# A hybrid encoder layer on one core: a planner that charges engines for a change of start partition, with loops by halves and a new table

## The chip, the cores and the metric

The kernel runs on 1 core of a Trainium2 chip, as one program in one launch. The metric is the device time of that program in microseconds, as the median over several executions. Times of single instructions come from one profiled execution.

## The reference

One layer of a streaming encoder is computed for two request groups that share the weights: a prompt of 512 new frames and 32 further frames of a running stream with 1,024 cached keys. Both are stacked to 544 token columns, D_MODEL is 1024, everything is float32.

```python
xn = _rms_norm(x, p['norm1'])
q, k, v, iq, ik, iw, u, g_a, g_b = _split(xn @ p['w_in'], IN_SPLITS)
ik = _layer_norm(ik, p['idx_k_g'], p['idx_k_b'])
o_a = attend(q, iq, iw, k, v, ik)                       # top-256 (prompt: 128) keys by index score, softmax attention
y_b, shift_new, wkv_new = _rwkv_time_mix(u, shift_prev, wkv0, p)   # 8 heads, matrix state, one delta-rule step per token
merged = sigmoid(g_a) * (o_a @ p['w_oa']) + sigmoid(g_b) * (y_b @ p['w_ob'])
h = x + merged @ p['w_out']
hn = _rms_norm(h, p['norm2'])
h = h + (silu(hn @ p['w_gate']) * (hn @ p['w_up'])) @ p['w_down']
y = _rms_norm(h, norm_f)
```

The keys, values, index keys, the final matrix states and the last projected row are outputs too.

## The kernel before

All products with weights run as three matmuls each: weights and activations are split into a rounded high part and a low rest (`hi`, `lo`), and `hi*hi`, `hi*lo`, `lo*hi` are summed in PSUM (`gemm`, L279; the feed-forward's last product, L1332). `wblock` (L255 to L260) loads a block of weights of 512 KB by DMA from SP's queue, makes `hi` on ACT (L256) and `lo` on DVE (L260). Two raw buffers and three split buffers turn round. Token columns are handled in two halves of 272.

Before the feed-forward, small work with long chains of dependences lies between these products:

- The prologue (L296 to L341) loads the eight tiles of x, splits each (ACT L300, DVE L301), squares it (ACT L309), sums the squares (DVE L311, PE L316 and L317) and makes the normalised, split x. The first weight blocks, 24 and 25, are multiplied by x before it is normalised.
- `kv` projects keys and values, normalises the index keys (DVE, to L406) and transposes them (PE L432).
- `rwkv_prep` (P0 to P3, one for each pair of heads) makes from projected rows the operands of the delta rule. Two heads share the 128 partitions: head 0 (`e` = 0) lies in partitions 0 to 63, head 1 in 64 to 127, and many instructions of 64 or 32 partitions work on one half.
- `chain_step` (C0 to C3, nine steps for each pair) goes PE L1060, copies of its result by DVE (L1061, partitions from 0) and ACT (L1062, from 64), PE L1063, copies by DVE (L1064) and ACT (L1065), PE L1066, DVE L1069 or L1073, then the next step. All of a chain uses one PSUM bank, bank 7. At its end L1096 and L1099 make the outputs in the same bank, which ACT empties (L1100, L1102).
- `prompt_index` and `sample_index` (X, SI) find the top keys, `attend_prompt` and `attend_sample` (A, AS) attend to them.

No engine's order is that of the source. `build` writes the program once in the order of `ORDER`, `plan` takes from it the instructions, their dependences and a priority for each, to which the table `SHIFT` adds an offset by group (a group is a step of `ORDER`, its weight blocks have a "w" ahead of the name), and `schedule` runs a list planner: it keeps a time for each engine, a duration for each instruction (`cost`), a delay from engine to engine (`HOP`), a rule for the array of PE (`Array`), and always takes the ready instruction of the lowest priority number. The order that comes out is what `program` builds the second time, with every wait as the dependences require. `SHIFT` also has "hold" and "keep", which are added to the priority of matmuls that use the array in another shape than the last one.

```python
best = min(((h[0][0] + (extra if x != array.shape else 0), x) for x, h in tiles.items() if h), default=None)
...
k = heapq.heappop(here[e])[1]
...
end = free[e] = began + work[k]
...
r = began if e == engine[s] == "PE" else end + HOP[e, engine[s]]
```

Of the kernel before, what the change touches and what calls it, by code (L numbers as in the profile page):

```python
# [35 lines left out]
def _consts():  # L36
# [34 lines left out]
SHIFT = {  # L71
# [7 lines left out]
    "wstart": -38300,  # L79
# [77 lines left out]
class Kernel:  # L157
# [646 lines left out]
    def rwkv_prep(self, P):  # L804
# [46 lines left out]
        for src, pc, ts in pieces(kn):  # L851
            pv = PB[:, pc, ts]
            for e in range(2):
                ps = heads[e][1]
                nc.vector.scalar_tensor_tensor(at_slot(AR, pc, ts, e)[ps], src[ps], -1.0, pv[ps], op0=OP.mult, op1=OP.mult)
        for src, pc, ts in pieces(r):
            nc.vector.tensor_tensor(at_slot(AR, pc, ts, 2), src, PB[:, pc, ts.start + 1:ts.stop + 1], op=OP.mult)
        for (src, pc, ts), (iv, _, _) in zip(pieces(tm), pieces(pi)):
            for e, ps, _ in heads:
                nc.vector.scalar_tensor_tensor(at_slot(BK, pc, ts, e)[ps], src[ps], 0.5, iv[ps], op0=OP.mult, op1=OP.mult)  # L860
# [34 lines left out]
        for cs in ([0], [1, 2, 3, 4], [5, 6, 7, 8]):  # L895
# [8 lines left out]
            for e, ps, po in heads:  # L904
# [10 lines left out]
                if cs[0]:  # L915
                    pq = slice(64 * e, 64 * e + 32)
                    nc.scalar.activation(M21[pq, u0:u0 + n], bv[pq, :, ac + 32:ac + 64], AF.Copy)
# [552 lines left out]
def unlayout(r):  # L1470
# [8 lines left out]
HOP = {("PE", "Activation"): 200, ("PE", "DVE"): 200, ("PE", "Pool"): 225, ("DVE", "PE"): 149, ("Activation", "PE"): 123, ("Pool", "PE"): 174,  # L1479
       ("Activation", "DVE"): 142, ("DVE", "Activation"): 128, ("DVE", "Pool"): 155, ("Activation", "Pool"): 170, ("Pool", "Activation"): 75,  # L1480
       ("Pool", "DVE"): 70, ("DVE", "DVE"): 127, ("Pool", "Pool"): 104, ("Activation", "Activation"): 60, ("PE", "PE"): 0}
SECOND = {"PE": 54, "Activation": 70, "DVE": 70, "Pool": 48, "SP": 0}
ENGINES = ("PE", "Activation", "DVE", "Pool", "SP")
# [11 lines left out]
def cost(i):  # L1495
# [19 lines left out]
    if engine == "Pool":  # L1515
        if i.opcode == "TensorTensor":
            spread = any(st == 0 and c > 1 for st, c in list(a[1].ap)[1:]) or (a[0].ap == a[1].ap and str(a[0])[:30] == str(a[1])[:30])
# [3 lines left out]
    if i.opcode == "StreamTranspose":  # L1521
        return 1.95 * n
# [5 lines left out]
    return (0.521 if half else 1.042) * n + 68 + (61 if len(aps) > 3 or (len(aps) == 3 and wide == 2 and n > 1) else 0)  # L1528

# [66 lines left out]
def plan(K, instructions):  # L1596
# [25 lines left out]
    return L, group, prio, succ, need, engine, dma, work, bundles(succ, group, engine, work, reach)  # L1622
# [24 lines left out]
def schedule(L, group, prio, succ, need, engine, dma, work, runs):  # L1647
# [6 lines left out]
    hold, keep = SHIFT.get("hold", 0), SHIFT.get("keep", 0)  # L1654
    names = [e for e in ENGINES if e in engine]
    free, order, here = dict.fromkeys(names, 0.0), {e: [] for e in names}, {e: [] for e in names}
# [6 lines left out]
    array, queue, bus, left = Array(), 0.0, 0.0, len(L)  # L1663
# [22 lines left out]
    while left:  # L1686
# [3 lines left out]
        while coming and coming[0][0] <= t + 1e-6:  # L1690
# [3 lines left out]
            else:  # L1694
                heapq.heappush(here[engine[k]], (prio[k], k))
        for e in names:
            while (here[e] or e == "PE") and free[e] <= t + 1e-6:
# [83 lines left out]
```

## Time and profile before

| what | value |
|---|---|
| median of 3 runs | 1024.93 us (1021.34 to 1025.96) |
| profiled execution, its own time | 1024.11 us |
| its span, first to last instruction | 1022.3 us |
| PE busy | 976.9 us, 96% of the span |
| DVE busy | 632.0 us, 62% |
| ACT busy | 461.4 us, 45% |
| POOL busy | 185.9 us, 18% |
| mean DMA rate | 110 GB/s over the span |

PE is the matmul engine, PEld its weight loads, DVE the vector engine, ACT the scalar engine, POOL GpSimd; SP issues nearly all DMAs. Busy time is the union of an engine's instructions. An instruction's record reaches from its start to the acknowledged write of its result, so the records of neighbours on one engine can overlap. "Idle before" is the time since the engine's last record ended, and the name behind an arrow is the instruction whose end let it go on.

### The profile page before, as it was taken

The page shows a single profiled execution, that of the slowest core. Times are in us where ns is not written, and L with a number is a line of the kernel's source. Part 1 is how long each engine was busy: PE and PEld are TensorE (multiplying, and loading weights), DVE is VectorE, ACT ScalarE, POOL GpSimd, SP SyncE. Part 2 cuts the span into 40 slices and gives each one's busy share as a digit, 9 for nine tenths or more (in the row PEclk, how much of TensorE's full clock was granted, in tenths as well). Part 3 has the DMA queues.
Part 4 walks back from the last instruction along what each step waited for, and adds up shares of the span by engine and source line. Part 5 has one row for each costly group of instructions (what it writes and reads, how often), then busy time and mean ns, then how long its engine had stood idle before and what let it go on. Part 6 is the DMA issues. An engine that isn't in the chain of part 4 may idle for free.

```text
span 1022.3 us, 20851 instructions
## 1 busy us (share of the span) xinstructions
PE 976.9 (96%) x8268; PEld 926.3 (91%) x8268; DVE 632.0 (62%) x1452; ACT 461.4 (45%) x965; POOL 185.9 (18%) x307
## 2 busy tenths in 40 slices
PE   6999999999989899999999999999999999999996
PEld 6989987888788788898889999999999999999995
DVE  6857536889989889799868564444444444323232
ACT  6643554665554686466644443223322233223231
POOL 2213113323232331031000131111111111001112
PEclk9999999999999999999999999999999999999998
DMA  6335332324143437442446422222233222232322
GB/s 231 91 116 185 105 99 72 115 99 142 42 137 113 133 98 209 129 118 75 145 142 179 170 83 83 83 94 93 83 85 100 85 83 83 73 98 77 95 73 88
DMA packets 63283, 112.58 MB, mean 110 GB/s; under 512 B 13617, under 2 KB 33873, under 8 KB 63057
## 3 DMA queue, kind: packets, MB, share of 16 engines
q1 hardware_dynamic: 62144, 110.72, 35.4%
q8 instruction: 65, 1.06, 0.4%
q10 hardware_dynamic: 1040, 0.52, 0.2%
q14 instruction: 34, 0.27, 0.1%
HBM read 93.67 MB, written 17.14 MB: 108 GB/s over the span
## 4 chain that ended last, share of the span: by engine, by line
PE 55%; DVE 7%; ACT 3%; issue 1%; DMA 0%; POOL 0%; SPq 0%; DVEq 0%; ACTq 0%
PE bank L279 38%; PE bank L1332 13%; DVE f L616 1%; DVE f L611 1%; DVE f L615 1%; PE bank L661 1%; DVE w L260 1%; PE bank L670 1%; PE bank L458 1%; DVE f L645 0%; DMA f<-gate_dram 0%; ACT f L649 0%; ACT f L604 0%; PE bank L459 0%; ACT k L452 0%
## 5 line engine op out<-in xcount | busy, mean ns | idle before, releaser
L279 PE MATMUL bank<-r,w 128*128 128x272 f32 x4752 | 653.9, 292 | 2.5 <-DVE f L1196 1.4
L279 PEld LDWEIGHTS bank<-r,w 128*128 128x128 f32 x4752 | 614.3, 189 | 9.4 <-issue 1.8
L256 ACT ACTIVATE w<-raw 128x1024 fp32r<-128x1024 f32 (+2 forms) x135 | 137.5, 1021 | 230.6 <-PE bank L279 173.8
L260 DVE TENSOR_TENSOR w<-raw,w 128x1024 fp32r<-128x1024 f32 (+2 forms) x135 | 176.4, 1308 | 95.9 <-ACT w L256 95.5
L1332 PE MATMUL bank<-r,w 128*128 128x272 f32 x1056 | 133.0, 288 | 0.0
L1332 PEld LDWEIGHTS bank<-r,w 128*128 128x128 f32 x1056 | 132.4, 188 | 0.0
L1310 POOL TENSOR_TENSOR f<-f 128x544 f32<-128x544 f32 x22 | 30.4, 1382 | 233.9 <-DVE f L1307 224.9
L1307 DVE TENSOR_TENSOR f<-bank,f 128x272 f32<-128x272 f32 x44 | 19.4, 441 | 74.8 <-PE bank L279 74.8
L1300 DVE TENSOR_TENSOR f<-bank,f 128x272 f32<-128x272 f32 x44 | 19.1, 435 | 45.0 <-PE bank L279 45.0
L458 PE MATMUL bank<-k 128*128 128x512 f32 (+5 forms) x102 | 37.8, 378 | 4.0 <-ACT f L604 2.9
L453 POOL TENSOR_TENSOR k<-f,k 64x512 fp32r<-64x512 f32 (+1 forms) x22 | 29.6, 1345 | 61.1 <-ACT k L452 55.2
L1334 DVE TENSOR_TENSOR f<-bank,f 128x272 f32<-128x272 f32 x16 | 7.1, 441 | 48.1 <-PE bank L1332 48.1
L611 DVE SCALAR_TENSOR_TENSOR f<-f,f 128x256 f32<-128x256 f32 (+2 forms) x45 | 31.8, 707 | 3.4 <-ACT f L604 2.4
L459 PE MATMUL bank<-k 128*128 128x512 f32 (+5 forms) x102 | 33.0, 332 | 0.0
L1336 ACT ACTIVATE f<-f 128x272 f32<-128x272 f32 x16 | 6.8, 423 | 57.5 <-DVE f L1334 57.5
L279 PE MATMUL bank<-k,w 128*128 128x272 f32 x144 | 25.3, 341 | 7.4 <-ACT k L300 6.2
L1338 POOL TENSOR_TENSOR f<-f 128x272 f32<-128x272 f32 x13 | 12.1, 934 | 111.1 <-ACT f L1336 103.0
L1301 ACT ACTIVATE f<-f 128x272 f32<-128x272 f32 x44 | 18.6, 424 | 30.0 <-DVE f L1300 30.0
L1252 POOL TENSOR_TENSOR f<-f 128x272 f32<-128x272 f32 x14 | 12.5, 894 | 108.0 <-ACT f L1250 108.0
L458 PEld LDWEIGHTS bank<-k 128*128 128x128 f32 x102 | 19.0, 188 | 13.8 <-ACT f L604 5.2
L279 PEld LDWEIGHTS bank<-k,w 128*128 128x128 f32 x144 | 23.2, 232 | 8.9 <-ACT k L300 6.2
L1076 POOL COPY f<-f 64x64 f32<-64x64 f32 x56 | 16.4, 294 | 66.8 <-DVE f L1073 64.9
(352 smaller groups left out, 1247.7 us busy)
## 6 DMA issues: line engine op xcount, KB each, us to landing
raw<-in_w_x_dram SPq DMA_DIRECT2D x41, 512.0 KB, 3.5
raw<-in_w_gate_dram SPq DMA_DIRECT2D x22, 512.0 KB, 3.6
raw<-in_w_up_dram SPq DMA_DIRECT2D x22, 512.0 KB, 3.6
raw<-in_w_down_dram SPq DMA_DIRECT2D x16, 512.0 KB, 3.6
gate_dram<-f SPq DMA_DIRECT2D x16, 272.0 KB, 2.5
raw<-in_w_oa_dram SPq DMA_DIRECT2D x8, 512.0 KB, 4.0
raw<-in_w_out_dram SPq DMA_DIRECT2D x8, 512.0 KB, 4.2
f<-iq_dram SPq DMA_DIRECT2D x26, 128.0 KB, 3.0
```

The source lines that it names most:

```text
L256: nc.scalar.activation(hi[:, a], raw[:, a], AF.Copy)
L260: self.lo_eng.tensor_tensor(lo[:, b], raw[:, b], hif[:, b], op=OP.subtract)
L279: nc.tensor.matmul(o, a[:, k], c[k][:, s], start=n == 0, stop=n == 3 * nk - 1)
L453: nc.gpsimd.tensor_tensor(ql[0:64], raw[0:64], qh_r.v(512)[0:64, :n], op=OP.subtract)
L458: nc.tensor.matmul(out, q[0][:, i:i + m], self.KS[:, j, keys], start=True, stop=False)
L459: nc.tensor.matmul(out, q[1][:, i:i + m], self.KS[:, j, keys], start=False, stop=stop)
L611: nc.vector.scalar_tensor_tensor(acc, r[:, i * S:(i + 1) * S], w, acc, op0=OP.mult, op1=OP.add)
L1300: nc.vector.tensor_tensor(t1[:, s], o, self.rs[:, s], op=OP.mult)
L1301: nc.scalar.activation(t1[:, s], t1[:, s], AF.Silu)
L1307: nc.vector.tensor_tensor(t2[:, s], o, self.rs[:, s], op=OP.mult)
L1310: nc.gpsimd.tensor_tensor(t1, t1, t2, op=OP.mult)
L1332: nc.tensor.matmul(o, a[:, k], c[k0 + k][:, s], start=m == 0, stop=m == 65)
```

## The change

- `side` gives the partition at which an instruction's output starts. `schedule` keeps the last such partition for ACT, DVE and POOL (`at`), and adds `TURN` (128, 110 and 112 ns) to an instruction's time where it differs. Ready instructions are kept in one heap for each side; an extra offset "turn" for another side exists in the code, but the table has no such entry, so it is 0.
- Delays from ACT to PE, ACT to POOL and POOL to ACT are raised. The planner's duration of a DVE transpose falls from 1.95 ns to 1.05 ns a column plus 84, and one form of POOL's multiplication is no longer taken as cheap.
- Three loops of `rwkv_prep` run over the partition halves first: the outputs to `AR` by half 0, then half 1, those to `BK` by half 1, then half 0, and the copy to `M21` behind the first copy of its half.
- All offsets of `SHIFT` are new (two lines of it stand for the table).

```diff
 SHIFT = {
-    "A0": 302900, "A1": -69100, "A2": 1141800, "A3": -1027600, "AS": -334800, "C0": 205900, "C1": -554900, "C2": -13000,
+    "A0": 230600, "A1": -4400, "A2": -703900, "A3": -225600, "AS": -582700, "C0": 247900, "C1": -1362900, "C2": -248200,
...
-    375100, "R1": -279800, "R2": -224600, "R3": 7200, "S": -56600, "SI": 103300, "U0": 10100, "U1": 1219400, "U2": 195800,
+    "R0": 299400, "R1": -1861400, "R2": -142400, "R3": 126400, "S": -59800, "SI": 126900, "U0": -21700, "U1": 1680300, "U2":
...
-        for src, pc, ts in pieces(kn):
-            pv = PB[:, pc, ts]
-            for e in range(2):
-                ps = heads[e][1]
+        for e, ps, _ in heads:
+            for src, pc, ts in pieces(kn):
+                pv = PB[:, pc, ts]
                 nc.vector.scalar_tensor_tensor(at_slot(AR, pc, ts, e)[ps], src[ps], -1.0, pv[ps], op0=OP.mult, op1=OP.mult)
...
-        for (src, pc, ts), (iv, _, _) in zip(pieces(tm), pieces(pi)):
-            for e, ps, _ in heads:
+        for e, ps, _ in heads[::-1]:
+            for (src, pc, ts), (iv, _, _) in zip(pieces(tm), pieces(pi)):
...
-                if cs[0]:
-                    pq = slice(64 * e, 64 * e + 32)
-                    nc.scalar.activation(M21[pq, u0:u0 + n], bv[pq, :, ac + 32:ac + 64], AF.Copy)
+                    if cs[0] and sh == 0:
+                        nc.scalar.activation(M21[pq, u0:u0 + n], bv[pq, :, ac + 32:ac + 64], AF.Copy)
...
-HOP = {("PE", "Activation"): 200, ("PE", "DVE"): 200, ("PE", "Pool"): 225, ("DVE", "PE"): 149, ("Activation", "PE"): 123, ("Pool", "PE"): 174,
-       ("Activation", "DVE"): 142, ("DVE", "Activation"): 128, ("DVE", "Pool"): 155, ("Activation", "Pool"): 170, ("Pool", "Activation"): 75,
+HOP = {("PE", "Activation"): 200, ("PE", "DVE"): 200, ("PE", "Pool"): 225, ("DVE", "PE"): 149, ("Activation", "PE"): 160, ("Pool", "PE"): 174,
+       ("Activation", "DVE"): 142, ("DVE", "Activation"): 128, ("DVE", "Pool"): 155, ("Activation", "Pool"): 210, ("Pool", "Activation"): 250,
+TURN = {"Activation": 128, "DVE": 110, "Pool": 112}
...
-        return 1.95 * n
+        return 1.05 * n + 84
...
+def side(i):
+
+    a = next((x for x in i.outs if hasattr(x, "ap")), None)
+    step = list(a.ap)[0][0] if a is not None else 0
+    return a.offset // step if step else 0
...
-                    k = heapq.heappop(here[e])[1]
+                    best = min(((h[0][0] + (turn if x != at[e] else 0), x) for x, h in here[e].items() if h), default=None)
+                    if best is None:
+                        break
+                    k = heapq.heappop(here[e][best[1]])[1]
...
+                    if sides[k] != at[e]:
+                        began += TURN[e]
+                        at[e] = sides[k]
                     end = free[e] = began + work[k]
```

The same instructions remain on every engine, the number of changes of PE's array shape is 150 before and 149 now, and the changes of an output's start partition go from 142 to 126 on DVE, from 235 to 231 on ACT and from 92 to 94 on POOL. From the product with `w_ob` on (`merge`, the second half of the span) the engines' orders are the same but for a few neighbours. Three places where the order moved (code from L1060 on has numbers lower by 2 in the changed file):

**SP's queue at the start of the program.** `raw` is a weight block, half of one where it says 128x512, x_t the eight tiles of x, cache_keys keys that a later step needs. Before:

```order
L225 DMA f_58<-in_vec_dram 128x80
L255 DMA raw<-in_w_x_dram 128x512
L296 DMA f_58<-in_x_t_dram 128x544 x4
L298 DMA f_58<-in_consts_dram 128x494
L255 DMA raw<-in_w_x_dram 128x512
L296 DMA f_58<-in_x_t_dram 128x544 x4
L439 DMA f_74<-in_cache_keys_dram 128x512 x2
L255 DMA raw<-in_w_x_dram 128x1024
```

Now:

```order
L255 DMA raw<-in_w_x_dram 128x1024
L439 DMA f_74<-in_cache_keys_dram 128x512 x2
L225 DMA f_58<-in_vec_dram 128x80
L255 DMA raw<-in_w_x_dram 128x512
L296 DMA f_58<-in_x_t_dram 128x544 x4
L298 DMA f_58<-in_consts_dram 128x494
L255 DMA raw<-in_w_x_dram 128x512
L296 DMA f_58<-in_x_t_dram 128x544 x4
```

The second weight block (512 KB) and two pieces of the key cache (256 KB each) moved ahead of everything that the first products need. On ACT, the square of a tile (L309) now often stands ahead of its split (L300), and on PE the first sum of squares (L316) stands behind 43 products of the first two blocks instead of 58.

**PE in a step of chain C1** (bank_89 is bank 7, the chain's; L279 are the products that stand between). Before:

```order
L279 MATMUL bank_83<-r_70,w 128x272 x2
L1063 MATMUL bank_89<-f_58,f_74 128x64
L279 MATMUL bank_83<-r_70,w 128x272
L1066 MATMUL bank_89<-f_74 128x128
L279 MATMUL bank_83<-r_70,w 128x272 x3
```

Now:

```order
L1061 MATMUL bank_89<-f_58,f_74 128x64
L530 LDWEIGHTS f_74
L530 MATMUL bank_86<-f_74 128x2
L279 MATMUL bank_82<-r_70,w 128x272 x8
L1064 MATMUL bank_89<-f_74 128x128
L279 MATMUL bank_82<-r_70,w 128x272 x4
```

Between the chain's second and third matmul of this step stand 8 products where 1 stood.

**PE at the end of chain C2**, where the outputs' second group of blocks begins (L1096, now L1094) and needs the bank that ACT is emptying. Before:

```order
L1099 MATMUL bank_89<-f_58,f_74 64x64 x2
L458 MATMUL bank_84<-k 128x256
L459 MATMUL bank_84<-k 128x256
L279 MATMUL bank_83<-r_70,w 128x272
L279 MATMUL bank_82<-r_70,w 128x272 x3
L1096 MATMUL bank_89<-f_74,f_58 64x128 x2
```

Now:

```order
L1097 MATMUL bank_89<-f_58,f_74 64x64 x4
L1094 MATMUL bank_89<-f_74,f_58 64x128
L1097 MATMUL bank_89<-f_58,f_74 64x64 x2
L279 MATMUL bank_82<-r_70,w 128x272 x13
L1094 MATMUL bank_89<-f_74,f_58 64x128 x2
```

Between the two groups stand 13 products where 4 and two score matmuls stood.

## Rows read from the trace of the kernel before

**Rows 1.** Stretches: length; busy (instructions) of PE, PEld, DVE, ACT, POOL; clock; DMA share; GB/s.

```profile
0.00:25.00 25.00, 17.04 (x97) 15.24 (x98) 15.93 (x28) 17.03 (x26) 6.70 (x26) 0.95 0.68 234
...
233.00:306.00 73.00, 67.61 (x706) 60.15 (x704) 66.31 (x233) 39.48 (x100) 22.41 (x54) 0.98 0.34 104
306.00:414.00 108.00, 100.89 (x951) 89.80 (x949) 97.44 (x265) 71.19 (x188) 27.25 (x51) 1.00 0.46 142
...
538.00:1000.00 462.00, 462.00 (x3686) 461.86 (x3685) 204.87 (x286) 144.69 (x226) 55.99 (x50) 1.00 0.31 95
1000.00:1022.30 22.30, 12.56 (x105) 12.08 (x103) 5.54 (x16) 3.53 (x8) 5.45 (x7) 0.86 0.30 101
sum 1022.30, PE 976.93 PEld 926.30 DVE 631.96 ACT 461.37 POOL 185.94; mean PE 122.12 PEld 115.79 DVE 78.99 ACT 57.67 POOL 23.24
```

**Rows 2.** Waits of PE: who waited for whom, us in total, times, longest.

```profile
PE bank L1066 <- ACT f L1065: 4.5, 9, 0.9
PE bank L1063 <- ACT f L1062: 3.0, 4, 1.3
...
PE bank L432 <- DVE f L406: 2.4, 2, 1.9
PE bank L1096 <- ACT f L1102: 1.8, 3, 1.1
...
PE bank L1060 <- DVE f L1073: 1.4, 1, 1.4
```

**Rows 3.** Timeline, all engines, 280.5 to 283 us: start, duration, instruction.

```profile
280.23 0.43 PE L1063 MATMUL bank<-f,f 128*128 128x64 f32 x2
...
281.31 0.22 ACT L1065 ACTIVATE f<-bank 64x64 f32<-64x64 f32 x1
...
281.55 0.49 ACT L762 ACTIVATE f<-bank,f 128x272 f32<-128x272 f32 x1
...
281.58 0.49 PE L1066 MATMUL bank<-f 128*128 128x128 f32 x2 [0.73 <-ACT f L1065]
```

**Rows 4.** Timeline, all engines, 393.3 to 396 us.

```profile
394.83 0.25 ACT L1102 ACTIVATE f<-bank 32x128 f32<-32x128 f32 x1
...
395.13 0.44 PE L1096 MATMUL bank<-f,f 128*64 128x128 f32 x4 [1.12 <-ACT f L1102]
```

**Rows 5.** Timeline of DVE alone, 476.5 to 479 us.

```profile
476.73 0.29 DVE L1069 SCALAR_TENSOR_TENSOR f<-f,f,bank 64x64 f32<-64x64 f32 x1
477.05 0.09 DVE L616 MATCH_VALUE_LOAD f<-f 128x8 f32 x1
477.15 0.69 DVE L616 MATCH_REPLACE8 f<-f 128x512 f32<-128x512 f32 x1
477.76 0.16 DVE L650 RECIPROCAL f<-f 128x2 f32<-128x2 f32 x1
477.94 0.56 DVE L645 CUSTOM_DVE_ANT_0 f<-bank,f 128x384 f32<-128x384 f32 x1
```

**Rows 6.** Stretches of the start (columns as in the first group).

```profile
0.00:3.00 3.00, 0.00 (x0) 0.00 (x0) 0.67 (x8) 1.49 (x2) 2.26 (x19) 1.00 0.26 73
3.00:6.00 3.00, 0.00 (x0) 0.00 (x0) 1.12 (x3) 1.25 (x2) 1.59 (x3) 1.00 0.94 307
6.00:9.00 3.00, 2.82 (x9) 2.30 (x10) 1.96 (x3) 2.51 (x5) 0.00 (x0) 1.00 0.99 341
25.00:29.00 4.00, 4.00 (x19) 4.00 (x19) 3.59 (x6) 1.69 (x3) 0.87 (x2) 0.50 0.31 114
```

**Rows 7.** Timeline, all engines, 0 to 30 us.

```profile
5.38 0.75 ACT L300 ACTIVATE k<-f 128x544 fp32r<-128x544 f32 x1 [0.38 <-DMA f<-in_x_t_dram]
6.03 0.64 ACT L309 ACTIVATE f<-f 128x544 f32<-128x544 f32 x1
...
6.18 9.18 PE L279 MATMUL bank<-k,w 128*128 128x272 f32 x44 [6.18 <-ACT k L300]
...
19.02 0.28 PE L316 MATMUL bank<-f 128*128 128x2 f32 x2
```

More of the change, by code (lines that the diff above doesn't have):

```diff
@@ L71 @@
 SHIFT = {
[7 rows of a table removed]
-    "wstart": -38300,
[7 rows of a table added]
+    17100, "wstart": -230000,
 }
@@ L1516, in cost @@
         if i.opcode == "TensorTensor":
-            spread = any(st == 0 and c > 1 for st, c in list(a[1].ap)[1:]) or (a[0].ap == a[1].ap and str(a[0])[:30] == str(a[1])[:30])
+            spread = any(st == 0 and c > 1 for st, c in list(a[1].ap)[1:])
             return 164.0 * n + 300 if "pow" in str(i.op) else (1.67 if spread else 2.1) * n + 130
@@ L1621, in plan @@
     engine, dma, work = [str(i.engine)[11:] for i in L], [i.opcode == "DMACopy" for i in L], [cost(i) for i in L]
-    return L, group, prio, succ, need, engine, dma, work, bundles(succ, group, engine, work, reach)
+    sides = [0 if x or e in ("PE", "SP") else side(i) for x, e, i in zip(dma, engine, L)]
+    return L, group, prio, succ, need, engine, dma, work, bundles(succ, group, engine, work, reach), sides
 def bundles(succ, group, engine, work, reach):
@@ L1644, in bundles, with schedule @@
     return runs
-def schedule(L, group, prio, succ, need, engine, dma, work, runs):
+def schedule(L, group, prio, succ, need, engine, dma, work, runs, sides):
     need, shared = list(need), [port(i) for i in L]
@@ L1653, in schedule @@
             members.setdefault(b, []).append(k)
-    hold, keep = SHIFT.get("hold", 0), SHIFT.get("keep", 0)
+    hold, keep, turn = SHIFT.get("hold", 0), SHIFT.get("keep", 0), SHIFT.get("turn", 0)
     names = [e for e in ENGINES if e in engine]
-    free, order, here = dict.fromkeys(names, 0.0), {e: [] for e in names}, {e: [] for e in names}
+    free, order, here = dict.fromkeys(names, 0.0), {e: [] for e in names}, {e: {} for e in names}
     for k, ks in enumerate(succ):
@@ L1662, in schedule @@
     ready, coming, times = [500.0] * len(L), [(500.0, k) for k in range(len(L)) if not need[k]], [500.0]
-    array, queue, bus, left = Array(), 0.0, 0.0, len(L)
+    array, queue, bus, left, at = Array(), 0.0, 0.0, len(L), dict.fromkeys(names, 0)
     before, mark, seen, rings = [[] for _ in L], [None] * len(L), {e: {} for e in names}, [0] * 8
@@ L1694, in schedule @@
             else:
-                heapq.heappush(here[engine[k]], (prio[k], k))
+                heapq.heappush(here[engine[k]].setdefault(sides[k], []), (prio[k], k))
         for e in names:
-            while (here[e] or e == "PE") and free[e] <= t + 1e-6:
+            while free[e] <= t + 1e-6:
                 if e == "PE":
```

10 rows, old and new, of the table SHIFT are left out of this document.

## Prediction, made before the changed kernel ran

> **What bounds the kernel now.** First I read the stretches [rows 1]. From 538 to 1000 us PE is busy for 462.00 of 462.00 us. That is 3,686 matmul records, 0.125 us each, with the clock at its full 2.4 GHz: the output projection and the feed-forward run at the pace of PE, and nothing an order does can shorten them. Over the whole span PE is busy for 976.93 of 1022.30 us, so all its idle time is 45.37 us, 4.4%. Of it 7.96 us lie in the first 25 us and 9.74 us behind 1000 us (the final norm). What is left, 45.37 - 7.96 - 9.74 = 27.67 us, is spread from 25 to 538 us, where the small work stands between the products: 5.39 us from 233 to 306, 7.11 us from 306 to 414. There DVE is busy for 66.31 of 73 us (91%) and 97.44 of 108 us (90%): PE bounds this half as well, but DVE has little room.
>
> Next I read who keeps PE waiting [rows 2]. The waits are many and short. The chain's own steps lead: 4.5 us in nine waits of L1066 for ACT's copy L1065, 3.0 us in four of L1063 for L1062, 1.8 us in three of L1096, 1.4 us in one of L1060. Together that is 10.7 us, or 39% of the 27.67. So the kernel loses time where PE comes to a chain matmul some tenths of a microsecond before ACT or DVE have its operand. That is what a planner does that takes those copies for shorter than they are.
>
> **Does a change of partition cost what the planner will charge?** On DVE [rows 5], L650 starts at 477.76, 0.08 us before L616 ends (477.15 + 0.69 = 477.84); both write from partition 0, so the records overlap. L1069 writes the upper half and ends at 477.02, and L616 behind it, from 0, starts at 477.05: a gap of 0.03 us. A change costs 0.08 + 0.03 = 0.11 us, and 110 ns is the new charge. On ACT [rows 3], L1065 (from partition 64) ends at 281.53 and L762 (from 0) starts at 281.55: a gap there too. So the charge is real, and the old planner thought every such copy in a chain step done about 0.1 us too early.
>
> One pair of rows shows a cost without a change of the output: L645 starts 0.02 us behind the end of L650 (477.92) [rows 5]. Both write from 0, but L645 reads PSUM from 0 where the last reader of PSUM, L1069, read from the upper half. The Trainium skill ("VectorE: DVE Perf Modes", section on two Vector instructions with no wait between them) says that an instruction is held until the earlier ones have finished when the start quadrant of its output, or of any input, differs from the last one in the same memory. The trace agrees in this pair, and by that rule the new charge leaves out holds that come from inputs alone; what that would do is rival 4.
>
> **The change part by part.**
>
> *The three loops.* DVE has 16 changes fewer, 142 to 126. At 0.11 us [rows 5] that is 1.8 us of DVE time, in P0 to P3. PE has products to run meanwhile, so I count 0. If DVE's pace set the end there, since it is 90% busy [rows 1], all 1.8 us would be gained: between -1.8 and 0.
>
> *The start.* Three DMAs with 0.52 + 0.52 = 1.05 MB now go ahead of everything. Before, the first tile of x was in use at 5.38 us [rows 7], by when 73 GB/s for 3 us and 307 GB/s for 2.38 us [rows 6] had moved 0.22 + 0.73 = 0.95 MB. Now 2.00 MB must move: 0.22 + 0.92 = 1.14 MB by 6 us, and the other 0.86 MB at 341 GB/s [rows 6] take 2.5 us, so the tile is there at 8.5 us. ACT then squares it first (0.64 us) and splits it (0.75 us) [rows 7], and PE starts at 9.9 instead of 6.18 us, 3.7 us late. Not all of it is lost, for ACT sets the pace behind it: before the sums of squares can start it has eight squares and six splits left, 8 x 0.64 + 6 x 0.75 = 9.6 us, so they start at about 18.1 us, hardly before the 19.02 of now [rows 7]. By then PE has done 43 products instead of 58. The debt is 15 products: 1.9 us at 0.125 us each [rows 1], or 3.2 us at half clock (4.00 us for 19 from 25 to 29 us, clock 0.50, 1.2 GHz [rows 6]). I take +1.9, because full speed is the commoner state, with ends 0 (the sums start 0.9 us earlier, and the second weight block is ready when the tiles come) and +3.7.
>
> *The chains.* At the place in C1, PE did one product between L1063 and L1066 and then waited 0.73 us for L1065 [rows 3]. Now 8 products stand there, 7 x 0.125 = 0.88 us more, and the wait is covered. At the end of C2, L1096 waited 1.12 us for L1102 [rows 4]. Now 13 products stand there where 4 and two score matmuls stood: at least (13 - 6) x 0.125 = 0.88 us more, and 0.24 us of the wait stays. So 1.61 of 1.85 us go at these two, 87%. Not so everywhere: in C0, and in some steps of C1, as many matmuls stand between as before, or fewer. I take less than half of that share of the 10.7 us, 40%: -4.3 us. The ends are -10.7 (every one of these waits) and +2 (new ones, below).
>
> *All other places.* 27.67 - 10.7 = 17.0 us of PE's idle time are other waits. Some gaps in the order grew, others shrank: in the key stage the transposes L432, which wait 2.4 us [rows 2], now follow each other sooner, two score matmuls of X1 stand closer to the ones whose bank they reuse, and one step of C1 and one of P2 lost what stood between. With four to six such places at 0.3 to 0.5 us each (the mean of L1066's waits is 4.5 / 9 = 0.5 us) they give back about 2.0 us; I take the gains elsewhere, most from 306 to 414 us, at 2.5 us. Net -0.5, between -4 and +3.
>
> *The table's offsets for the second half, the final norm.* The orders there are the same. 0.
>
> **The sum** is against the profiled execution's 1024.11 us (1.81 us over its span): 1024.1 + 0 + 1.9 - 4.3 - 0.5 = 1021.2 us. The median of the runs shown, 1024.93, is 0.8 us above the profiled one, so that this is 0.36% under the median. A measurement of this kernel can tell about 0.5%, or 5.1 us, from no change: faster means under 1019.8, slower over 1030.1.
>
> **The rivals.**
>
> 1. *The waits go almost all.* If the lengthened delays and the charge fit the chip, 80% of the chain's waits go, 0.8 x 10.7 = 8.6 us, with the same loss at the start and the other 0.5: 1024.1 + 1.9 - 8.6 - 0.5 = 1016.9. For it: the price measured above is the charge. Against it: DVE at 90%, whose queue is not made shorter by a better guess of one copy.
>
> 2. *The waits only move.* A chain matmul that comes later makes the next step later, and each chain has nine steps in a row behind each other. If what is saved at one copy comes back at L458, L432 or L530, the chain term is 0, and with the gain and loss of the other terms (+1.9, -0.5) the time is 1025.5. For it: nearly the same number of switches and of side changes on ACT and POOL as before.
>
> 3. *Slower: the start.* All 3.7 us of the late start are lost, and PE, which idles for tiles, falls to half clock once more. The trace shows the stretch 25 to 29 us at clock 0.50, behind 7.96 us of idle time in the first 25 [rows 1, 6]; 4 us there hold 19 records instead of 32, so a stretch of 7 us loses 2.8 us. With no gain in the chains: 1024.1 + 3.7 + 2.8 = 1030.6. It decides when start and clock cost over 6 us and the chains give nothing. Against it: ACT's pace, not PE's, sets the sums. The Trainium skill ("Perfetto Trace Analysis", Matmul Optimizations) says that the engine's power follows its use, so that matmuls should come in unbroken batches; these rows agree.
>
> 4. *Half the charge.* Holds that come from inputs alone stay uncharged [rows 5], so PE still comes too early wherever DVE or ACT copy from the other half of a bank. If these are behind half of the chain's waits, the chain term is -2.1: 1024.1 + 1.9 - 2.1 - 0.5 = 1023.4.
>
> **How the numbers follow.** Forecast 0.42 (its own range 1017 to 1025), rival 1 0.25, rival 2 0.20, rival 3 0.06, rival 4 0.07. Faster by over 0.5% is rival 1 but for a little (0.24) and a third of the forecast's range (0.15): 0.39 with nothing from the others. Slower is two thirds of rival 3 (0.04) and tails of rivals 2 and 4 (0.04): 0.08. The rest, 0.53, is within 0.5%. The range: below 1014.5 lies the part of rival 1 in which chain and other waits both come to their lower ends (0.10), above 1028 rival 3 and the tail of rival 2 (0.09).
>
> **What would show it.** The waits of L1064 for L1063 (L1066 and L1065 now) should sum to 2 to 3 us instead of 4.5, and PE's idle time from 25 to 538 us to about 23 us instead of 27.7. PE's first matmul should start at 9 to 10 us, the sums of squares near 18 us. DVE's busy time should stay within 2 us, and 538 to 1000 us should be full as before. I am wrong if idle time from 25 to 538 us does not fall, or if the first 50 us lose more than 4 us.

## The result, and the profile after

The changed kernel ran in 1009.92 us (median of 4, 1007.27 to 1012.05), the kernel before beside it in 1024.08 us: a ratio of 0.9863, 95% interval 0.9824 to 0.9901. The forecast was 1021.2 us with 1014.5 as its lower end, so the direction was right and the size a fifth of what came (2.9 us of 14.2). The profiled execution took 1007.89 us with a span of 1006.1, so 16.2 us less than the profiled one of before.

The page's first part says where to look. The first line is PE's, 12.0 us below the 976.9 of before with the same 8,268 records:

```profile
PE 964.9 (96%) x8268; PEld 923.4 (92%) x8268; DVE 628.1 (62%) x1452; ACT 460.0 (46%) x965; POOL 190.4 (19%) x307
```

The stretches of the changed kernel answer to [rows 1]. Since the product with `w_ob` starts 16.3 us earlier, the last two stretches are taken 16.2 us earlier:

```profile
0.00:25.00 25.00, 15.17 (x93) 14.66 (x94) 13.92 (x27) 15.44 (x25) 7.24 (x26) 0.93 0.66 231
233.00:306.00 73.00, 67.02 (x751) 60.43 (x743) 70.99 (x238) 40.82 (x103) 25.81 (x53) 1.00 0.35 112
306.00:414.00 108.00, 104.06 (x972) 93.13 (x973) 95.68 (x274) 74.06 (x198) 29.82 (x51) 0.97 0.48 146
521.80:983.80 462.00, 462.00 (x3687) 462.00 (x3687) 204.18 (x285) 144.69 (x225) 56.32 (x50) 1.00 0.31 94
983.80:1006.10 22.30, 12.53 (x103) 11.93 (x101) 5.55 (x16) 3.52 (x8) 5.45 (x7) 0.79 0.30 101
```

The second half is what it was: 3,687 records in 462.00 us. All of the gain lies ahead of it. The same view from 25 us to the start of that product, first of the kernel before, then of the changed one:

```profile
25.00:538.10 513.10, 485.43 (x4387) 437.22 (x4387) 405.61 (x1122) 296.23 (x707) 117.80 (x224) 0.99 0.39 118
```

```profile
25.00:521.80 496.80, 475.22 (x4392) 434.82 (x4391) 404.49 (x1124) 296.37 (x709) 121.39 (x224) 0.98 0.40 123
```

The stretch is 16.3 us shorter for the same work (4,387 and 4,392 records). PE's idle time in it went from 513.10 - 485.43 = 27.67 us to 496.80 - 475.22 = 21.58 us: 6.1 us. The other **10.2 us came out of PE's busy time**, although PE stood at half clock for 20.5 us up to here where it had stood for 13.7. PEld tells it better: its idle time fell from 75.88 to 61.98 us, by 13.9 us.

How can the same matmuls be busy for 10 us less? The groups of PE by line in the two stretches, before:

```profile
L458 PE MATMUL bank<-k 128*128 128x512 f32 (+5 forms) x102 | 37.8, 378 | 4.0 <-ACT f L604 2.9 <-ACT k L452 0.8 <-DVE f L665 0.2
L1066 PE MATMUL bank<-f 128*128 128x128 f32 x72 | 15.6, 298 | 4.7 <-ACT f L1065 4.5
L902 PE MATMUL bank<-f 64*128 64x128 f32 x144 | 13.8, 292 | 2.2 <-DVE f L875 1.3 <-ACT f L914 0.5 <-ACT f L917 0.2
L1063 PE MATMUL bank<-f,f 128*128 128x64 f32 x54 | 10.7, 280 | 3.2 <-ACT f L1062 3.0
```

and after, where L902, L1066 and L1063 are L901, L1064 and L1061:

```profile
L458 PE MATMUL bank<-k 128*128 128x512 f32 (+5 forms) x102 | 35.8, 359 | 3.1 <-DVE f L645 1.3 <-ACT f L604 1.0 <-ACT k L452 0.6
L1064 PE MATMUL bank<-f 128*128 128x128 f32 x72 | 14.8, 288 | 0.3 <-ACT f L1063 0.3
L901 PE MATMUL bank<-f 64*128 64x128 f32 x144 | 11.6, 289 | 0.8 <-ACT f L913 0.8
L1061 PE MATMUL bank<-f,f 128*128 128x64 f32 x54 | 9.8, 263 | 2.9 <-ACT f L1060 2.9
```

A record lasts some 290 ns, at full pace a new one starts every 125 ns, so two or three lie over each other. PE may stand for 150 ns and no idle time appears, because the last record is still open. (The end of a matmul's record is modelled by the profile and no acknowledged write; the starts are measured.) [Rows 3] hold such a case: L1063's two records are followed by one of L279, the last before L1066:

```profile
280.48 0.37 PE L279 MATMUL bank<-r,w 128*128 128x272 f32 x1
```

It ends at 281.58 - 0.73 = 280.85 us. From its start to that of L1066 1.10 us passed where 0.125 are needed. The loss is 0.98 us, the idle time shown 0.73. I took every record up to the output projection from start to start against the spacing of undisturbed records. The waits with visible idle time, 76 before and 51 now, lost 11 to 14 us beyond that idle time and now lose 8 to 9, by which records are taken for undisturbed; in every such count it is 3 to 5 us less. How the rest of the 10.2 us divides between waits that show no idle time and slower records depends on that choice, and stays open. The Trainium skill ("Perfetto Trace Analysis", section "Identifying the Most-Contended Engine") says that a matmul's busy share is a poor measure of the distance to the roofline, for matmuls are pipelined, and that the busy share of the weight loads is a good one. PE's 96% before and 96% after, beside PEld's 91% and 92%, agree.

Who keeps PE waiting now, against [rows 2]:

```profile
PE bank L432 <- DVE f L406: 4.0, 3, 3.2
PE bank L1061 <- ACT f L1060: 2.9, 4, 1.6
PE bank L279 <- ACT f L762: 2.8, 2, 2.2
PE bank L530 <- DVE f L529: 1.7, 5, 0.5
...
PE bank L1094 <- ACT f L1100: 0.4, 1, 0.4
...
PE bank L1064 <- ACT f L1063: 0.3, 1, 0.3
```

The chain's waits went from 10.7 to 2.9 + 0.4 + 0.3 = 3.6 us; L1058's idle time is 0.2 us in all. All others together stand at 21.58 - 3.6 = 18.0, before 17.0.

The place of [rows 3] is instructive, the timeline of all engines in that step of C1:

```profile
279.49 0.43 PE L1061 MATMUL bank<-f,f 128*128 128x64 f32 x2 [0.92 <-ACT f L1060]
...
280.03 0.87 ACT L762 ACTIVATE f<-bank,f 128x272 f32<-128x272 f32 x2
...
280.57 1.27 PE L279 MATMUL bank<-r,w 128*128 128x272 f32 x8 [0.64 <-ACT f L762]
...
281.69 0.38 PE L1064 MATMUL bank<-f 128*128 128x128 f32 x2
```

L1064 doesn't wait, as forecast from the eight products ahead of it. But the products themselves wait 0.64 us for ACT's L762, which now stands ahead of the chain's copy, and L1061 waits 0.92: this step lost more than before. At the place of [rows 4] the wait of 1.12 us is gone altogether:

```profile
365.37 1.90 PE L279 MATMUL bank<-r,w 128*128 128x272 f32 x13
...
366.83 0.25 ACT L1100 ACTIVATE f<-bank 32x128 f32<-32x128 f32 x1
...
367.20 0.44 PE L1094 MATMUL bank<-f,f 128*64 128x128 f32 x4
```

The start, against [rows 7], by the timelines of PE and ACT:

```profile
8.40 0.66 ACT L309 ACTIVATE f<-f 128x544 f32<-128x544 f32 x1
...
9.75 1.05 PE L279 MATMUL bank<-k,w 128*128 128x272 f32 x3 [9.75 <-ACT k L300]
...
17.43 0.28 PE L316 MATMUL bank<-f 128*128 128x2 f32 x2
```

The largest single move is chain C2. Its first and last matmuls on PE, before and after:

```profile
313.91 0.39 PE L1060 MATMUL bank<-f 128*128 128x128 f32 x2
...
388.31 0.39 PE L1066 MATMUL bank<-f 128*128 128x128 f32 x2
```

```profile
311.61 0.39 PE L1058 MATMUL bank<-f 128*128 128x128 f32 x2
...
362.33 0.38 PE L1064 MATMUL bank<-f 128*128 128x128 f32 x2
```

The same nine steps take 50.7 us instead of 74.4. C0 and C1 last 3.0 and 1.7 us longer than before. C3 starts at 396.7 instead of 412.9 us and takes 77.3 instead of 62.4, other work being set between its steps. C2 and C3 show two ways out of a wait. In C3, 334 PE records instead of 223 stand between a chain matmul and the next one of its step, and its visible waits for L1062 and L1065 (1.6 us) are gone, as the prediction has it. In C2 they are gone too (1.1 us), but with 224 records where 452 stood: here the copies come sooner, on average 1.1 us after each of the two matmuls instead of 2.1 and 1.9.

### The profile page after: what moved, and what is told of

It reads as the page before. It is cut to its first block, busy times and chain, and to the rows that moved or that the text cites. A ratio compares the mean times of both kernels' runs of the same rounds, so it can differ in the third digit from the quotient of the medians.

```text
span 1006.1 us, 20829 instructions
## 1 busy us (share of the span) xinstructions
PE 964.9 (96%) x8268; PEld 923.4 (92%) x8268; DVE 628.1 (62%) x1452; ACT 460.0 (46%) x965; POOL 190.4 (19%) x307
## 4 chain that ended last, share of the span: by engine, by line
PE 72%; DVE 14%; DMA 6%; ACT 4%; issue 2%; SPq 1%; POOL 0%; DVEq 0%; ACTq 0%; POOLq 0%
PE bank L279 49%; PE bank L1330 13%; PE bank L458 1%; DVE w L260 1%; DVE f L616 1%; PE bank L459 1%; DMA iq_dram<-f 1%; DMA raw<-in_w_x_dram 1%; DVE f L611 1%; DVE f L615 1%; PE bank L901 1%; DVE f L529 1%; ACT w L256 1%; PE bank L1058 1%; DVE f L928 1%
## 5 line engine op out<-in xcount | busy, mean ns | idle before, releaser
L279 PE MATMUL bank<-r,w 128*128 128x272 f32 x4752 | 658.3, 293 | 3.2 <-ACT f L762 2.8
L279 PEld LDWEIGHTS bank<-r,w 128*128 128x128 f32 x4752 | 617.3, 189 | 10.0 <-ACT f L762 3.5
L256 ACT ACTIVATE w<-raw 128x1024 fp32r<-128x1024 f32 (+1 forms) x135 | 137.8, 1021 | 223.6 <-PE bank L279 172.7
L260 DVE TENSOR_TENSOR w<-raw,w 128x1024 fp32r<-128x1024 f32 (+1 forms) x135 | 176.5, 1308 | 97.8 <-ACT w L256 97.6
L279 PE MATMUL bank<-k,w 128*128 128x272 f32 x144 | 22.8, 322 | 9.8 <-ACT k L300 9.8
L279 PEld LDWEIGHTS bank<-k,w 128*128 128x128 f32 x144 | 21.6, 219 | 10.1 <-ACT k L300 9.7
L458 PEld LDWEIGHTS bank<-k 128*128 128x128 f32 x102 | 19.1, 188 | 10.7 <-issue 5.1
L1074 POOL COPY f<-f 64x64 f32<-64x64 f32 x56 | 16.3, 292 | 65.3 <-DVE f L1071 63.9
```

What stands on the lines that cost most here:

```text
L256: nc.scalar.activation(hi[:, a], raw[:, a], AF.Copy)
L260: self.lo_eng.tensor_tensor(lo[:, b], raw[:, b], hif[:, b], op=OP.subtract)
L279: nc.tensor.matmul(o, a[:, k], c[k][:, s], start=n == 0, stop=n == 3 * nk - 1)
L458: nc.tensor.matmul(out, q[0][:, i:i + m], self.KS[:, j, keys], start=True, stop=False)
```

## The experiments

Sixteen kernels ran. "Chain waits" below is visible idle time of PE before L1060, L1063 and L1066 (9.4 us before, 3.2 after), "idle" PE's from 25 us to the output projection (27.7 and 21.6). Ratios are to the kernel before on the same chip, with 95% intervals.

### One part alone

**New charges and loops, old table.** The changed kernel with `SHIFT` of before.

```diff
 SHIFT = {
-    "A0": 230600, "A1": -4400, "A2": -703900, "A3": -225600, "AS": -582700, "C0": 247900, "C1": -1362900, "C2": -248200,
+    "A0": 302900, "A1": -69100, "A2": 1141800, "A3": -1027600, "AS": -334800, "C0": 205900, "C1": -554900, "C2": -13000,
...
```

> The changed kernel with the old table of offsets: new prices (side change, delays, durations) and the new loops remain. Price theory (a planner that knows what the copies cost brings PE to its operands later, whatever the table): most of the 14 us are here, 1010 to 1016 us. Table theory (the new offsets arrange the groups better): 1020 to 1028 us. Joint theory (a table is good only under the prices it was chosen for): 1018 us or more, and possibly slower than before.

Measured: 1050.41 us, 1.0262 (1.0230 to 1.0294). Chain waits 4.7 us, idle 45.6.

**New table, old charges and loops.** The kernel before with `SHIFT` of the change (the diff above, the other way round).

> The kernel before with the new table alone: old prices, old loops. Table theory: 1008 to 1014 us. Price theory: 1020 to 1028 us. Joint theory: 1018 us or more, and PE's visible idle time from 25 us to the end of the small work not under that of the kernel before (27.7 us).

Measured: 1043.46 us, 1.0187 (1.0154 to 1.0221). Chain waits 9.1 us, idle 40.0.

**The changed kernel without the charge for the partition.**

```diff
-TURN = {"Activation": 128, "DVE": 110, "Pool": 112}
+TURN = {"Activation": 0, "DVE": 0, "Pool": 0}
```

> The changed kernel with the charge for a side change set to 0 on all three engines; raised delays, durations, loops and the new table remain. If the side charge carries the gain: 1018 us or more, and PE's waits for copies of the chain (L1063 for L1064, L1060 for L1061 and the like) back at 8 to 11 us. If the delays and the table carry it: 1008 to 1013 us, those waits at 4 to 6 us.

Measured: 1038.84 us, 1.0143 (1.0109 to 1.0176). Chain waits 11.3 us, idle 38.9.

**The loops alone**, in the kernel before (the loops of the diff above).

> The kernel before with the three loops by halves alone. All theories: no change that can be told, 1019 to 1029 us; 1.8 us less time on DVE between its instructions at most. If the loops carried part of the gain after all: 1016 us or less.

Measured: 1035.07 us, 1.0119 (1.0081 to 1.0157). Chain waits 8.1 us, idle 33.0.

What follows: the charge does to the chain's waits what the prediction said. Under either table they are 3 to 5 us with it and 8 to 11 without. But none of the parts is faster alone, each is 1 to 3% slower, and low chain waits go with the worst time here (the first run). Table, charges and program belong together, which is the joint theory of the expectations. The loops' 1035 us lie outside what every theory had for them, 1019 to 1029.

Part of these losses goes with the granted clock. Its median over the executions was 0.969, 0.984, 0.985 and 0.981, in the kernel before beside them 0.989. Over 67 executions of the kernel before, 0.01 less went with 6.8 us more (last section), so that an estimate of 14, 4, 3 and 6 of the 28, 21, 16 and 12 us lost belongs to it. By that estimate each part alone would still be slower without it.

### Is the table a knife's edge?

Every offset of the table 1% up or down, in the changed kernel and in the kernel before.

```diff
+SHIFT = {k: int(v * (1.01 if n % 2 else 0.99)) for n, (k, v) in enumerate(SHIFT.items())}
```

> The changed kernel with each offset of its table raised or lowered by 1%, in turn. If the new prices make orders good in themselves (price theory): within 5 us of the changed kernel, 1007 to 1015 us. If a table is a single good point in rough ground (joint theory): 1015 to 1040 us.

> The kernel before with each offset of its table raised or lowered by 1%, in turn. Price theory: the old orders are no worse off for it, 1020 to 1030 us. Joint theory: 1026 to 1045 us, and PE's waits for the chains' copies at 8 to 11 us as in all orders made without the side charge.

Measured: 1006.64 us, 0.9830 (0.9804 to 0.9856), and 1025.40 us, 1.0016 (0.9995 to 1.0037). These two can't answer the question: 1% moves no instruction. The planner's lists for them are those of the change and of the kernel before, entry for entry on every engine, and the traces show the same sequence of lines, all 8,268 records of PE included. They are repetitions. As such they say that the change gains as much on another chip, and that one program measured twice differs by 0.2 to 0.3%, so that 0.3% between two medians is no difference. Whether other orders are as good, the last two runs of this section say.

### The start

The changed kernel with the start of before (SP's queue, prologue, key stage's first block), and the reverse; the entries of the engines' lists that belong to the start are put into the other kernel's order.

```diff
-schedule(*plan(K, instructions)))[0]
+begin(schedule(*plan(K, instructions))))[0]
```

> The changed kernel, but the instructions up to the first 255 matmuls (loads of x and of the first blocks, norm, first products) stand in the old order in their places on every engine. If the new start is a loss of 1.9 us, as forecast: 1007 to 1009 us, 1.9 us under the changed kernel. If the start is a gain of 1.5 us, as the times at which the 255th matmul starts say (48.1 us before, 46.6 us after): 1010.5 to 1013 us.

> The kernel before with the new order of the same first instructions. If the new start is a loss of 1.9 us: 1025 to 1027 us. If a gain of 1.5 us: 1020 to 1023.5 us, with the first matmul at 9.8 us and yet the 255th at about 46.6 us.

Measured: 1010.80 us, 0.9867 (0.9844 to 0.9890), and 1027.41 us, 1.0031 (1.0010 to 1.0052). To the kernel before, the new start is a loss of 3 us (1 to 5). To the change, the old start is one: the run with the shifted offsets, which is the changed program, took 1006.64 us on the same chip beside it, 4 us less (all its four executions lie below all five of this one). So each start fits its own kernel, and neither has a price by itself: the first run lies in the range expected of a gain, the second just above that of a loss. By matmuls in order, PE of the changed kernel is 3.6 us late at the first, 1.3 early at the 290th (50.7 for 52.0 us) and 0.7 late at the 480th (84.2 for 83.5): L432's wait, 2.4 us in [rows 2] and 4.0 now, takes the lead back. On the chip of these two runs, either exchanged start comes to the 480th matmul over 2 us behind the kernel's own: 84.2 for 82.1 us in the changed kernel, 83.7 for 81.3 in the kernel before.

### A table searched anew

Two tables found by a search on the planner's own estimate, both from the old table: one for the kernel before with the new loops and its own charges, one for the changed kernel (two offsets of the first stand for the tables).

```diff
 SHIFT = {
-    "A0": 302900, "A1": -69100, "A2": 1141800, "A3": -1027600, "AS": -334800, "C0": 205900, "C1": -554900, "C2": -13000,
+    "A0": -2403700,
+    "A1": 931600,
...
```

> New loops, old prices, and a table searched anew from the old one, by the planner's own estimate under the old prices (3,300 to 7,400 tables tried). If the new prices are what makes the orders better: 1018 to 1030 us, with 7 to 11 us of PE's waits for the chains' copies. If any further search gives as much (search theory): 1008 to 1016 us.

> The changed kernel's prices and loops, with a table searched anew from the old one (which alone gave 1050 us), by the planner's own estimate under the new prices, in the same time and from the same starting table. Price theory: at least 8 us under the run with old prices, 1008 to 1020 us, with 2 to 5 us of waits for the chains' copies. Search theory: within 5 us of the run with old prices.

Measured: 1027.09 us, 1.0033 (1.0007 to 1.0059), with chain waits of 10.5 us, and 1028.86 us, 1.0058 (1.0039 to 1.0077), with 6.2. Neither search reached the change, so these two can't say how much of the gain another table under the old charges could have. They lie within 5 us of each other, as the search theory had it, and the price theory's 1008 to 1020 us for the second were missed. But the second lost to the clock: its four executions had 0.967 to 0.970, the kernel before beside it 0.987 in the median, which by the 6.8 us above is an estimate of 13 us. One stretch of its profile shows it (columns as in [rows 1]):

```profile
236.70:264.00 27.30, 21.54 (x141) 18.42 (x140) 23.75 (x80) 10.50 (x27) 9.33 (x19) 0.50 0.15 42
264.00:541.40 277.40, 268.49 (x2435) 242.54 (x2435) 237.72 (x637) 171.78 (x415) 63.88 (x106) 0.99 0.43 130
```

For 27.3 us PE ran at half clock, 0.194 us a record, where the rest of that half has 0.114.

### The chain's waits taken away by hand

The kernel before, with PE's order alone edited: each chain matmul that waited visibly stands behind as many of the products that followed it as its wait took (26 places); then the other visible waits too (57 places).

```diff
-schedule(*plan(K, instructions)))[0]
+fill(schedule(*plan(K, instructions))))[0]
...
+def fill(order):
+    return {**order, "PE": [MOVED.get(j, k) for j, k in enumerate(order["PE"])]}
```

> The kernel before with one edit, by hand: on PE alone, each of the 26 chain matmuls that waited visibly in the profile of before (L1060, L1063, L1066, L1096) stands behind as many of the products that followed it as its wait took. Table, charges, loops and the orders of ACT, DVE, POOL and SP are those of before. The 26 show 12.5 us of idle time; from start to start they take 16.7 us more than a record's 0.125 us each. Theory A (PE came too early, and a wait costs more than the idle time it shows): 10 to 17 us less, 1007 to 1014 us, and PE busy falls by 2 us or more with the same records. Theory B (visible idle time is all there is): at most 12.5 us less, 1012 to 1016 us, with PE busy within 1 us of before. Theory C (waits only move, because a chain that starts a step later ends it later): 1020 to 1027 us, PE idle within 2 us of before's 27.7 from 25 us to the output projection. Theory D (the new order gains by its table, not by the chain's waits): less than 5 us won.

> As the run before it, and the other 31 visible waits of PE from 25 us to the output projection too (L458, L432, L902, L947, L1018, L530 and a few more; 12.5 us of idle time, 17.8 us from start to start), 57 places in all. Theory A: 10 us or more under the run before it, 995 to 1006 us. Theory B: 5 to 12 us under it. Theory C, for these places: within 4 us of it, since what waits there waits for DVE, whose queue is 90% busy and doesn't come sooner by what PE does.

Measured: 1040.58 us, 1.0166 (1.0135 to 1.0196), and 1052.88 us, 1.0277 (1.0246 to 1.0308). None of the four theories had this: the chain's waits fell to 3.2 us, as low as in the changed kernel, and the kernel became 16 us **slower**. Waits of PE in the first of the two:

```profile
PE bank L279 <- ACT f L762: 6.2, 4, 2.3
PE bank L530 <- DVE f L529: 5.2, 6, 2.9
...
PE bank L661 <- ACT f L652: 2.5, 3, 1.5
...
PE bank L1060 <- DVE f L1073: 2.2, 5, 0.9
```

L279's waits for L762 were 0.7 us before. PE's time did not vanish, it moved. What stands behind it shows in DVE's waits for the chain's matmuls from 160 to 450 us, of the kernel before and of this run:

```profile
DVE f L1061 <- PE bank L1060: 2.7, 1, 2.7
...
DVE f L1073 <- PE bank L1066: 1.9, 2, 1.6
...
DVE f L1069 <- PE bank L1066: 1.4, 1, 1.4
...
DVE f L1064 <- PE bank L1063: 0.2, 1, 0.2
```

```profile
DVE f L1064 <- PE bank L1063: 4.8, 3, 2.9
DVE f L1061 <- PE bank L1060: 4.1, 3, 2.7
DVE f L1069 <- PE bank L1066: 3.9, 1, 3.9
DVE f L1073 <- PE bank L1066: 3.4, 4, 1.7
```

DVE stood 16.2 us for them instead of 6.2. Its queue is in order: where the chain matmul comes later, its copy on DVE comes later, and what stands behind that copy with it, which then can be late for PE. The same stretch as a whole, of the kernel before, of this run, and of the changed kernel:

```profile
160.00:450.00 290.00, 269.96 (x2600) 238.33 (x2600) 253.82 (x763) 173.04 (x434) 84.12 (x157) 0.99 0.38 117
```

```profile
160.00:450.00 290.00, 259.69 (x2496) 229.05 (x2493) 240.03 (x738) 160.50 (x410) 77.99 (x150) 0.96 0.36 111
```

```profile
160.00:450.00 290.00, 274.23 (x2673) 247.26 (x2672) 264.35 (x800) 180.74 (x455) 87.24 (x161) 0.98 0.40 123
```

All engines did less in it than before (PE 2,496 records for 2,600), and in the changed kernel more (2,673). The second row also has the lowest clock, 0.96: half clock for 20.5 us of the stretch, 3.4 before. Over all executions the median clock was 0.981 for 0.989 beside it, an estimate of 5 of the 16 us. The change fills PE and DVE both.

### The chain earlier

PE's order alone again, now the other way: the second and third chain matmul of all 36 steps 4 places earlier, in the kernel before and in the changed one (same edit, another `MOVED`).

> The kernel before with PE's order alone edited: the chain's second and third matmuls (L1063, L1066) of all 36 steps each stand 4 products earlier (70 of 72 by 4 or 2 matmuls or more). Theory A (the chain paces the stretch from 210 to 420 us through DVE, whose next work hangs on it): the chains get shorter, their waits on PE grow to 15 us or more, and yet the time is the same or up to 8 us less: 1016 to 1026 us. Theory B (PE's idle time paces): 72 waits of up to 0.5 us more, 10 to 30 us slower: 1034 to 1054 us.

> The changed kernel with PE's order alone edited in the same way: L1061 and L1064 of all 36 steps stand 4 products earlier. Theory A (the chain paces, the waits are no loss): 1005 to 1014 us, within 4 us of the changed kernel, though the chain's waits grow from 3 to 15 us or more. Theory B (the products in front of the chain's matmuls are what the change gave): most of the 15 us is lost again, 1020 to 1030 us or more.

Measured: 1040.13 us, 1.0155 (1.0112 to 1.0198), with chain waits of 20.5 us; and 1020.70 us, 0.9951 (0.9931 to 0.9971), with 10.2. In the changed kernel four products in front of each chain matmul, half a microsecond, are worth 9.0 us of the 14 by the ratios (5 to 13), 10.8 by the medians. The clock doesn't explain it: its median was 0.985, in the change 0.983. The stretch from 160 to 450 us of that run, whose profiled execution was its slowest (1024.25 us, clock 0.981):

```profile
160.00:450.00 290.00, 270.61 (x2568) 239.34 (x2568) 252.01 (x763) 173.55 (x434) 85.74 (x158) 0.96 0.38 117
```

These are nearly the numbers of the kernel before, 2,568 records where it had 2,600. Theory B holds in both: the chain does not pace the half by itself. With the runs above, a chain matmul must come neither before its copy is there (PE stands, openly or within its records) nor long after (DVE stands). The place that is right hangs on the order of the other queues: the changed kernel's places were planned together with them, those set by hand were not.

### More search, and holds from inputs

The changed kernel's table searched on under its own charges, and under a charge for every change of the start quadrant of inputs and outputs within one memory, with a dearer strided transpose.

```diff
-                    if sides[k] != at[e]:
+                    reads, writes = sides[k]
+                    if any(at[e].get((c, m), v) != v for c, xs in enumerate((reads, writes)) for m, v in xs):
                         began += TURN[e]
...
-        return 1.05 * n + 84
+        return (1.05 if len(list(a[0].ap)) < 4 else 1.9) * n + 84
```

> The changed kernel, its table searched further under its own charge, as a control for the run behind it. If more search under these prices gives more: 1005 us or less. If the table was at the end of what the planner's prices can tell: 1006 to 1014 us.

> The changed kernel with the charge for every change of the start quadrant of an input or an output within one memory (SBUF or PSUM), the price of a strided transpose raised to 1.9 ns a column, and its table searched under these prices. If holds from inputs alone cost as much as the part that the change charges (rival 4 of the prediction): 1003 us or less, and chain waits of 2 us or less. If they cost little: 1006 to 1016 us, as the control.

Measured: 1008.17 us, 0.9850 (0.9802 to 0.9899), and 1011.38 us, 0.9869 (0.9831 to 0.9907), the latter with chain waits of 4.3 us. Neither differs from the change by more than one program does from itself. Charging inputs brings nothing that a measurement can tell. These two answer the question about the knife's edge: in the first, 1,002 of PE's 7,429 places hold another instruction than in the change, in the second 2,916, and the time is the same. So the gain doesn't hang on one lucky order. Both tables were picked by a search on the planner's estimate, under a charge; a table moved at random was not run.

## Why the prediction was wrong in size

**The step that failed** is in the first paragraph: that all an order can win is PE's idle time, and that 27.67 us of it is "what is left". By that the chain's term was idle time times a share. PE's busy time was taken as fixed work. It isn't: 10.2 of the 16.3 us came out of it, which no term of the sum could hold. PEld stood beside it in [rows 1], with 73 - 60.15 = 12.85 us idle from 233 to 306 us where PE shows 5.39, and I didn't ask why. That waits inside the records shrank is shown for the records behind visible waits (3 to 5 us); for the rest it is only argued.

Step by step, in the prediction's order:

- *538 to 1000 us is fixed*: right, 462.00 of 462.00 us.
- *PE bounds this half as well, but DVE has little room*: the second part was wrong. From 160 to 450 us DVE went from 87.5% to 91.2% busy. The objection to rival 1, that a better guess of one copy doesn't shorten DVE's queue, missed that DVE waits as well, for the chain's matmuls alone 6.2 us there, and 4.3 in the changed kernel.
- *A change of partition costs 0.11 us and the charge is real*: held. The two pairs it was read from are typical: among neighbours with less than 80 ns between them in the trace of before, the median goes from an overlap of 77 ns to a gap of 31 ns on DVE where the output's start changes (129 times), from 96 to 24 ns on ACT (178 times). Taking the charge out brings the chain's waits from 3.2 to 11.3 us.
- *The loops, 0*: not measured by themselves. In the old table they cost 12 us, about 6 of it with a lower clock; that the rest is the table's misfit and not the loops' price is argued, not shown. DVE's busy time fell by 3.9 us, not within 2.
- *The start, +1.9*: its mechanism was right (first matmul at 9.75 us, forecast 9.9; sums at 17.43, forecast 18.1), its price was not a price of the start alone. In the kernel before, the new start loses 3 us (1 to 5), which holds the 1.9; in the changed kernel the old one loses 4.
- *The chains, -4.3*: half of the mechanism was right and the size too small. Their visible waits lost 7.1 us, 66% and not 40%; L1064's are 0.3 us where 2 to 3 were forecast. Of the two places it was read from, one gave all and one took 0.83 us more (0.92 + 0.64 for 0.73). My 40% came from counting products between the chain's matmuls, but a wait goes also where the copy comes sooner, as in C2, which no excerpt of PE's order shows.
- *Other places, -0.5*: +1.0 in idle time. Idle time from 25 us on was forecast at about 23 us and is 21.6.
- *Rival 1* (1016.9 us) came nearest in cause and still lay 7 us too high, for the same failed step. *Rival 2* described what the hand-filled order does, not what the planner does, which moves the other queues too: C2 became shorter. *Rival 3*: no loss of 3.7 us by the start in the changed kernel. *Rival 4*: not seen in the run that charges inputs.

What is not settled is how the gain divides between the table and the charges. Each without the other is slower, and neither of my searches from the old table reached the change's time, so that a table as good under the old charges can't be excluded. Nor is the granted clock separated from the orders: it was lower in most of the slower kernels, and only its size could be estimated.

## What to carry to other kernels

Where matmul records overlap, take idle time from the weight loads, or from start to start, before you say how much an order can win: here the idle time on PE's own row showed 6 of 16 us. A wait on the busiest engine is not yet a loss that filling it will win back; ask what stands behind the consumer on the other in-order queues, and move all queues together. A planner's table and its prices are one thing: here the old table under the new prices was 2.6% slower than the kernel it came from. And before a small shift of a planner's input is called harmless, see whether it moved a single instruction.

## What the hardware showed unexpectedly

The same program varies with the granted clock. 67 executions of the kernel before, on five chips, went from 1019.8 to 1031.2 us at a mean clock of 0.994 to 0.979, and 0.01 less went with 6.8 us more (a line through all of them, correlation -0.87). The four of the change were 1007.3 and 1007.9 us at 0.987 and 0.985, but 1012.0 and 1012.1 us at 0.981 and 0.980. How long PE is idle doesn't tell the clock by itself: ahead of the output projection, the kernel before with its chain matmuls 4 places earlier and the run that charges inputs both stood at half clock for 27.3 us, with 36.5 and 22.0 us of idle time. The change has 20.5 us there and the kernel before 13.7, so it won in spite of its clock.
